# A hybrid attention and retention layer: queries and values stored whole, retention finished every 11 steps instead of 8, output norm weights multiplied on GpSimd

## The chip, the cores and the metric

The kernel runs on one core of one Trainium2 chip. The core has a matrix engine (TensorE, PE in the profile, with its weight loads as PEld), three engines for elementwise work (VectorE, DVE; ScalarE, ACT; GpSimd, POOL), a queue engine that issues transfers (SyncE, SP), and 16 DMA engines between DRAM and SBUF. The metric is the time of one execution on the device, in microseconds (us).

## The reference

One layer over 2048 rows of 1024 numbers, all in float32:

```python
h = rms_norm(x, norm_gain)
q_a, k_a, v_a, g_a, q_r, k_r, v_r, g_r, m_a, m_r = split_columns(h @ w_in)    # 1024 -> 7168
o_a = chunk_band_attention(q_a, k_a, v_a, rel_bias)     # 8 heads of 64, chunks of 64, 8 chunks to the left
branch_a = (o_a * silu(g_a)) @ w_out_attn
o_r = retention_chunkwise(rotary(q_r), rotary(k_r), v_r, gn_gain)   # 8 heads, keys of 64, values of 128
branch_r = (o_r * silu(g_r)) @ w_out_ret
mixed = sigmoid(m_a) * branch_a + sigmoid(m_r) * branch_r
out = rms_norm(x + mixed @ w_out, final_gain)
```

Retention is attention without a softmax: scores of queries and keys times a fixed decay mask, and beside them a running state per head, a 64 x 128 matrix, that is decayed and added to. Its result is normalised for each head.

## The kernel before

**Precision.** A matmul multiplies rounded float32 (fp32r). So an operand is *split*: a high part (an ACT copy that rounds) and a low part (a subtraction of the high part). Three products (high-high, high-low, low-high) stand for one. In names, `wh` and `wl` are the parts of a weight, `sh` and `sl` of masked scores, `o2h` and `o2l` of squares.

**The dense stream.** All projections run as one stream of small *steps*, three matmuls of 128 x 512 each. Blocks are multiplied by a scheme of seven products instead of eight; a product takes four steps, its PSUM tile is `ps_..._x` to `ps_..._z`, and DVE and ACT add these up in tiles `u` and `c` between the products. Weights are loaded on ACT's queue (`raw_g`, `raw_p`), sums of them are made on POOL (`t_g`, `t_p`), split into `wh` and `wl`.

**The stages.** The rows are worked on in two halves. In order: projection 0 (queries, keys and values of half 0), attention 0, retention 0, projection 1, attention 1, retention 1, and a last stage with the two branches' output projections (`ba0`, `br0`, `ba1`, `br1`), the merge, and `out` with the final norm. During attention and retention the gates' projection (`ps_g`) of that half is fed in between: `fill(n)` runs n steps of the dense stream. `later(n, fn)` puts a function off by n steps, `put(n, ...)` a store on SP; `sure()` runs put-off work early where something needs it. Until the last stage each engine works in the order in which the program emits its instructions; in the last stage a scheduler may move those of ACT, DVE and POOL.

**Queries and values on the way.** Projected queries and values are split at once, and both parts go to DRAM (`qrscr` line 176, `vrscr` line 178): `queries` (line 953) by way of `parted` (936), the low part on DVE; `ep_vr` (985) centres the values, then `high` (1003) on ACT and `low` (1007) on POOL.

**Retention** (main loop, lines 1557 to 1589). Heads go in four pairs p, a half's rows in four steps st of 256 rows: 16 units (p, st) per half, each of two heads i. `load_scored` (1373) loads keys and queries of a unit, both parts; `load_valued` (1397) the keys transposed and decayed (`kd`) and the values (`vr`), both parts; `load_state` (1412) takes up the state in half 1. Per head: `scores` (1424) gives `sr` by four matmuls, DVE multiplies by the mask (`sm`), ACT and POOL split it; `output` (1498) adds the products of state and scores into `o`; `evacuate` (1514) copies it out and squares it. Per unit, `update` (1453) multiplies keys and values into `kv`, and `added` (1465) adds it to `state` on DVE; for the first step of a pair ACT copies it there instead. Then ACT rounds the state into `sstk` and DVE adds the low part (1481, 1485). After the last step of half 0 state and sstk are stored (`sts`, `sks`). A fill of about two steps (`RET_FILLS`, line 60) stands between pieces. SBUF tiles come from a pool of 22 buffers.

**Finishing.** `finish_yr` (1071) loads one head's retention output, its gate and its norm factors, multiplies them on DVE and POOL, and stores them (`yrs`) for the branch's projection, which loads them as `r`. For half 1 this happens in the last stage, 16 times, one every `YR_EVERY` steps from step 14 on (lines 65, 66, 1720).

**Output.** `ep_out` (1153) adds the residual on DVE for a half row block of 128 x 512 (`xr`), squares and sums it on ACT, and when both halves are there makes the factor of the norm on DVE and multiplies row factor and norm weights (`fg`) in one DVE operation for each half (1173).

The main loop's body, which sets the order around the change:

```python
if i == 0:
    ops = ps_ret.tile(...)
    if st < 7:
        update(p, st)
    if m + 1 < len(todo):
        load_valued(*todo[m + 1])
        load_state(*todo[m + 1])
fill(RET_FILL)
...
output(p, st, i, parts.pop((p, st, i)), ops)
...
parts[items[n + 2]] = scores(*items[n + 2])
if i == 0 and m + 2 < len(todo):
    load_scored(*todo[m + 2])
fill(RET_FILL)
```

## Time and profile before

| | us |
|---|---|
| three runs: median (lowest, highest) | 1989.13 (1988.7, 1997.05) |
| the profiled execution, as timed | 1994.13 |
| its span in the profile | 1992.3 |
| PE busy in the span | 1927.1 |
| DVE busy | 1362.2 |
| ACT busy | 900.4 |
| POOL busy | 853.0 |

The mean granted clock of the matrix engine was 0.994 of full speed. In this execution retention 0 lies at about 590 to 765 us, projection 1 at 765 to 1105, retention 1 at 1394 to 1560, the last stage from 1560 on.

How to read the lines of the profile: `L140` is the line of a helper that issues most instructions, so that tiles tell them apart; `out<-in` are the tiles written and read. In a timeline a row has its start, its duration, the engine, and in brackets how long the engine idled before it and what ended that. `kv<-vr` is the update, `sr<-qr,kr` the scores, `o<-sh,vr` the output, `sm<-sr,dm` the mask. A wait row names the waiting instruction, what it waited for, and the sum, the number and the longest of these waits.

### The profile page before, as it was taken

Reading aid. Unit: us, or ns where it says so; the run is one execution under the profiler, and the core shown is the slowest. Engines: PE = TensorE matmul, PEld = TensorE weight load, DVE = VectorE, ACT = ScalarE, POOL = GpSimd, SP = SyncE. Lnnn points to the kernel's source line nnn. Section 1 sums busy time; section 2 is a strip of 40 time slices with the busy share of each in tenths; the row PEclk is TensorE's granted clock in tenths of the full one; section 3 lists DMA queues with packets and bytes.
Section 4 is the critical chain, followed back from the end, with each engine's and each line's share of the span. In section 5 each row is a group of like instructions: output and inputs, shape, how many; then the busy total and the mean of one; then the engine's idle time right before and its main releaser. Section 6 shows DMA issues by size and latency. Waiting matters only on the chain.

```text
span 1992.3 us, 30382 instructions
## 1 busy us (share of the span) xinstructions
PE 1927.1 (97%) x9712; PEld 1606.7 (81%) x9712; DVE 1362.2 (68%) x2613; ACT 900.4 (45%) x1827; POOL 853.0 (43%) x703
## 2 busy tenths in 40 slices
PE   6899999999999999999999999999999999999998
PEld 4677788888887877787788888888888887888886
DVE  7887878677765658889887677765557653544554
ACT  6454554566654545443333555654455311322221
POOL 2343544555546665555553444444665144021000
PEclk9999999999999999999999999999999999999999
DMA  4576795756549987687785646554998999976564
GB/s 148 156 265 186 226 307 196 213 153 183 161 132 268 289 243 250 214 289 230 231 277 173 190 150 176 157 144 141 275 285 283 334 377 360 341 242 216 193 193 138
DMA packets 341967, 447.45 MB, mean 225 GB/s; under 512 B 30808, under 2 KB 195312, under 8 KB 341808
## 3 DMA queue, kind: packets, MB, share of 16 engines
q1 hardware_dynamic: 284800, 389.92, 61.3%
q10 hardware_dynamic: 57008, 55.59, 9.2%
q8 instruction: 78, 1.28, 0.3%
q14 instruction: 81, 0.66, 0.1%
HBM read 294.50 MB, written 150.89 MB: 224 GB/s over the span
## 4 chain that ended last, share of the span: by engine, by line
PE 52%; DMA 6%; DVE 6%; issue 2%; POOL 1%; SPq 1%; ACT 0%; DVEq 0%; ACTq 0%; POOLq 0%
PE ps_g_z L140 4%; PE ps_g_x L140 4%; PE ps_p_z L140 3%; PE o L140 2%; PE po L140 2%; PE ps_p_x L140 2%; PE ps_g_v L140 2%; PE ps_g_w L140 2%; PE ps_g_y L140 2%; PE wide L140 2%; PE tp L140 1%; PE ps_p_y L140 1%; PE sr L140 1%; PE ps_p_w L140 1%; PE ps_p_v L140 1%
## 5 line engine op out<-in xcount | busy, mean ns | idle before, releaser
L140 POOL TENSOR_SCALAR pr<-pr,rsum 128x640 f32<-128x640 f32 (+4 forms) x128 | 96.0, 750 | 225.9 <-DVE ptl L140 105.7
L140 PE MATMUL ps_p_z<-r,wh_p 128*128 128x512 f32 x448 | 142.7, 400 | 7.0 <-DVE c_p L140 4.5
L140 PE MATMUL ps_g_z<-r,wh_g 128*128 128x512 f32 x448 | 143.9, 403 | 4.0 <-DVE c_g L140 4.0
L140 PE MATMUL ps_g_x<-r,wh_g 128*128 128x512 f32 x448 | 142.7, 400 | 1.9 <-ACT u_g L140 1.9
L140 PE MATMUL ps_p_x<-r,wh_p 128*128 128x512 f32 x448 | 142.3, 399 | 1.4 <-ACT u_p L140 1.4
L140 DVE CUSTOM_DVE_ANT_0 pr<-wide,bt 128x640 f32<-128x640 f32 (+4 forms) x128 | 94.3, 737 | 71.2 <-PE wide L140 65.4
L140 ACT ACTIVATE pr<-pr,mn 128x640 f32<-128x640 f32 (+4 forms) x128 | 98.0, 766 | 84.9 <-DVE mn L140 84.9
L140 POOL TENSOR_TENSOR t_p<-raw_p,t_p 128x512 f32<-128x512 f32 x50 | 74.5, 1491 | 130.1 <-DVE wl_p L140 114.9
L140 DVE TENSOR_TENSOR ptl<-tp,pth 128x384 fp32r<-128x384 f32 x168 | 96.0, 573 | 40.8 <-ACT pth L140 40.5
L140 ACT CAST pth<-tp 128x384 fp32r<-128x384 f32 x168 | 84.7, 516 | 70.0 <-PE tp L140 64.5
L140 DVE TENSOR_TENSOR wl_p<-t_p,wh_p 128x512 fp32r<-128x512 f32 x112 | 106.4, 951 | 2.0 <-ACT wh_p L140 2.0
L140 POOL TENSOR_TENSOR sl<-sm,sh 128x512 fp32r<-128x512 f32 x64 | 87.7, 1371 | 44.3 <-ACT sh L140 27.5
L1122 POOL TENSOR_TENSOR gr<-gr,ta 128x512 f32<-128x512 f32 x32 | 44.6, 1395 | 141.8 <-DVE gr L1121 133.3
L140 PEld LDWEIGHTS ps_p_z<-r,wh_p 128*128 128x128 f32 x448 | 82.5, 190 | 24.7 <-issue 7.2
L140 PEld LDWEIGHTS ps_p_x<-r,wh_p 128*128 128x128 f32 x448 | 83.8, 190 | 19.9 <-ACT u_p L140 2.2
L140 PE MATMUL wide<-ka,qa 128*128 128x512 f32 (+2 forms) x448 | 94.4, 326 | 2.3 <-DVE mn L140 2.3
L140 DVE TENSOR_TENSOR sm<-sr,dm 128x512 f32<-128x512 f32 x64 | 44.1, 690 | 71.9 <-PE sr L140 41.3
L140 PEld LDWEIGHTS tp<-ident,pr 128*128 128x128 f32 x560 | 71.3, 140 | 27.1 <-POOL pr L140 2.2
L140 POOL TENSOR_TENSOR wl_g<-t_g,wh_g 128x512 fp32r<-128x512 f32 x56 | 75.0, 1339 | 42.3 <-ACT wh_g L140 31.4
L140 PE MATMUL po<-pth,va 128*128 128x256 f32 x336 | 93.1, 298 | 0.0
L140 PE MATMUL tp<-ident,pr 128*128 128x128 f32 x560 | 89.0, 272 | 2.9 <-POOL pr L140 1.6
L140 ACT CAST wh_p<-t_p 128x512 fp32r<-128x512 f32 x112 | 69.1, 619 | 48.1 <-PE ps_p_z L140 19.5
(1184 smaller groups left out, 5879.2 us busy)
## 6 DMA issues: line engine op xcount, KB each, us to landing
raw_g<-in_w_in_dram ACTq DMA_DIRECT2D x56, 512.0 KB, 5.4
raw_p<-in_w_in_dram ACTq DMA_DIRECT2D x50, 512.0 KB, 6.4
qa<-qas SPq DMA_DIRECT2D x128, 128.0 KB, 3.1
qr<-qrs SPq DMA_DIRECT2D x128, 128.0 KB, 4.4
vr<-vrs SPq DMA_DIRECT2D x64, 256.0 KB, 5.3
ka<-kas SPq DMA_DIRECT2D x40, 256.0 KB, 3.7
va<-vas SPq DMA_DIRECT2D x40, 256.0 KB, 3.4
kds<-kdt_k SPq DMA_DIRECT2D x32, 256.0 KB, 4.4
```

The costliest lines, as they stand in the source:

```text
L140: return tc.keep_in_program_order(op(*a, **k))
L1122: pool.tensor_tensor(g, g, ta, ALU.add)
```

## The change

1. Queries and values are stored in DRAM whole, as plain float32, and loaded whole. The split is done in retention: an ACT copy some 7 or 8 steps after the load (`later(8 + more, high)`), a DVE subtraction two steps later, in place for the queries. Queries come as one tile for both heads (`qr`, with the high part `qh`); values as `vr`, split into `v_..._0` and `v_..._1`.
2. In the retention loop values are loaded two units ahead instead of one, and the load positions of queries and values trade places. `update` stands behind the fill, directly ahead of `output`. The first state of a pair is cleared by a POOL memset and then added to like the others; the rounding of the state into `sstk` is on DVE instead of ACT, directly behind the additions.
3. `YR_EVERY` goes from 8 to 11.
4. In `ep_out` POOL multiplies the residual sum by the norm weights beside ACT's square; the row factor is then applied by DVE for one half and by ACT for the other. The sum of the two squares and the added constant become one DVE operation. The last row block's first half is stored from ACT's queue.

The numbers of matmuls are the same, 9698 in both. DVE has 84 instructions more, ACT 29 more, POOL 4 more, SP issues 65 transfers fewer.

```diff
-YR_EVERY = 8
+YR_EVERY = 11
...
-    qrscr = [[D(f"qrs_{c}_{b}", [2, 4, 32, 2, 2, T], F32R) for b in range(NB)] for c in range(2)]
+    qrscr = [[D(f"qrs_{c}_{b}", [2, 2, 32, 2, 2, T]) for b in range(NB)] for c in range(2)]
-    vrscr = [[D(f"vrs_{h}_{b}", [P, 4, 2, DV], F32R) for b in range(NB)] for h in range(HEADS)]
+    vrscr = [[D(f"vrs_{h}_{b}", [P, 4, DV]) for b in range(NB)] for h in range(HEADS)]
...
     def queries(cc, b, xs, nm, late):
-        parted(xs, nm, late + 9, dve, lambda i, h: r32(qrscr[cc][b][:, :, :, h, i]).rearrange("u i c t -> (i c) u t"))
+        def store(n, i):
+            src = xs[n][32 * i:32 * i + 32].rearrange("c (u t) -> c u t", u=2)
+            dma(qrscr[cc][b][:, i // 2, :, n, i % 2].rearrange("u c t -> c u t"), src)
+
+        for n in range(2):
+            for i in range(4):
+                later(late + 8 + PUT + n, lambda n=n, i=i: store(n, i))
...
+                put(PUT, vrscr[h][b], vc)
-            def high():
-                vv.extend(two(f"vr_{nm}", (P, 4, DV)))
-                act.copy(vv[0], vc)
-
-            def low():
-                pool.tensor_tensor(vv[1], vc, r32(vv[0]), ALU.subtract)
-                for n in range(2):
-                    put(PUT, r32(vrscr[h][b][:, :, n, :]), r32(vv[n]))
-
             later(2, centred)
-            later(4, high)
-            later(6, low)
...
-        act.activation(junk, xr, AF.Square, accum_out=fs[:, i:i + 1])
+        act.activation(junk, xr, AF.Square, scale=DM ** -0.5, accum_out=fs[:, i:i + 1])
+        pool.tensor_tensor(fg, xr, fg, ALU.mult)
...
-        dve.tensor_reduce(ft, fs, AX.X, ALU.add)
-        dve.tensor_scalar(ft, ft, 1.0 / DM, NORM_EPS, ALU.mult, ALU.add)
+        dve.scalar_tensor_tensor(ft, fs[:, 0:1], NORM_EPS, fs[:, 1:2], ALU.add, ALU.add)
         rsqrt(ft, fr, tm, hv)
+        dve.tensor_scalar(halves_[1], halves_[1], fr, None, ALU.mult)
+        act.mul(halves_[0], halves_[0], fr)
         for f in range(2):
-            o, fg = halves_[f]
-            dve.scalar_tensor_tensor(o, o, fr, fg, ALU.mult, ALU.mult)
-            put(6, out[0, t * P:(t + 1) * P, 512 * f:512 * f + 512], o)
+            dst = out[0, t * P:(t + 1) * P, 512 * f:512 * f + 512]
+            if t == SEQ // P - 1 and not f:
+                act.dma_start(dst, halves_[f])
+            else:
+                put(6, dst, halves_[f])
...
+            def high():
+                qs.append(E(f"qh_{nm}", F32R, (P, 2, T)))
+                act.copy(qs[0], r32(ql))
+                later(2, low)
+
+            def low():
+                dve.tensor_tensor(ql, r32(ql), r32(qs[0]), ALU.subtract)
+                qs.append(ql)
+
+            later(8 + more, high)
...
+            def high():
+                ws = [E(f"v_{nm}_{i}", F32R, (P, 2, 2 * DV)) for i in range(2)]
+                for i in range(2):
+                    act.copy(ws[i][:, :, 0:DV], raw[:, i])
+                later(2, lambda: low(ws))
+
+            def low(ws):
+                for i in range(2):
+                    dve.tensor_tensor(ws[i][:, :, DV:2 * DV], raw[:, i], r32(ws[i][:, :, 0:DV]), ALU.subtract)
+                vs.extend(ws)
+
+            later(7 + more, high)
...
             def added():
                 for i in range(2):
-                    if st == 0:
-                        act.copy(state[:, i, :], kvv[0:64, i, 0:DV])
-                        continue
...
-                later(3, lambda: high(sstk))
-
-            def high(sstk):
-                act.copy(sstk[0:64], state)
-                later(1, lambda: low(sstk))
-
-            def low(sstk):
+                dve.tensor_copy(sstk[0:64], state)
                 dve.tensor_tensor(sstk[64:128], state, r32(sstk[0:64]), ALU.subtract)
...
-        load_scored(*todo[0])
-        load_valued(*todo[0])
-        load_scored(*todo[1])
+        load_scored(*todo[0], 3)
+        load_valued(*todo[0], 5)
+        load_scored(*todo[1], 5)
         load_state(*todo[0])
+        load_valued(*todo[1], 9)
+        load_scored(*todo[2], 9)
...
-                if st < 7:
-                    update(p, st)
                 if m + 1 < len(todo):
-                    load_valued(*todo[m + 1])
                     load_state(*todo[m + 1])
+                if m and m + 2 < len(todo):
+                    load_scored(*todo[m + 2])
             fill(RET_FILL)
+            if i == 0 and st < 7:
+                if st == 0:
+                    pool.memset(state, 0.0)
+                update(p, st)
...
-            if i == 0 and m + 2 < len(todo):
-                load_scored(*todo[m + 2])
+            if i == 1 and m + 2 < len(todo):
+                load_valued(*todo[m + 2])
             fill(RET_FILL)
```

DVE's order in retention 0, around unit (1, 1) (second head pair, second step), before. `c22`, `u3`, `u2` are sums of the gate projection, `wl` low parts of its weights; the last number of a name only tells tiles apart.

```order
L140 TENSOR_TENSOR c22_g0_9_7664<-ps_g0_9_z_7642,u3_g0_9_7614 128x512
L140 TENSOR_TENSOR wl_g0_10_0_7640<-raw_g0_10_0_7245,wh_g0_10_0_7639 128x512
L140 TENSOR_TENSOR sm_1_1_1_7689<-sr_1_1_1_7676,dm_1_1_7400 128x512
L140 SCALAR_TENSOR_TENSOR state_6975<-state_6975,kv_1_1_7706 64x128 x2
L140 TENSOR_TENSOR state_6975<-kv_1_1_7706,state_6975 64x256 x3
L140 TENSOR_TENSOR u3_g0_9_7614<-ps_g0_9_w_7698,u3_g0_9_7614 128x512
L140 TENSOR_TENSOR wl_g0_10_1_7694<-t2_g0_10_7499,wh_g0_10_1_7693 128x512
L140 TENSOR_TENSOR sm_1_2_0_7763<-sr_1_2_0_7743,dm_1_0_7395 128x512
L140 TENSOR_TENSOR sstk_1_1_7727<-state_6975,sstk_1_1_7727 64x256
```

And the same stretch after the change:

```order
L140 TENSOR_TENSOR c22_g0_9_7595<-ps_g0_9_z_7571,u3_g0_9_7537 128x512
L140 TENSOR_TENSOR wl_g0_10_0_7569<-raw_g0_10_0_7154,wh_g0_10_0_7568 128x512
L140 TENSOR_TENSOR sm_1_1_1_7625<-sr_1_1_1_7607,dm_1_1_7270 128x512
L140 TENSOR_TENSOR v_1_1_0_7588<-vr_1_1_7499,v_1_1_0_7588 128x2x128
L140 TENSOR_TENSOR v_1_1_1_7589<-vr_1_1_7499,v_1_1_1_7589 128x2x128
L140 TENSOR_TENSOR u3_g0_9_7537<-ps_g0_9_w_7634,u3_g0_9_7537 128x512
L140 TENSOR_TENSOR wl_g0_10_1_7630<-t2_g0_10_7418,wh_g0_10_1_7629 128x512
L140 TENSOR_TENSOR qr_1_2_7526<-qr_1_2_7526,qh_1_2_7650 128x512
L140 SCALAR_TENSOR_TENSOR state_6879<-state_6879,kv_1_1_7664 64x128 x2
L140 TENSOR_TENSOR state_6879<-kv_1_1_7664,state_6879 64x256 x3
L140 CAST sstk_1_1_7694<-state_6879 64x256
L140 TENSOR_TENSOR sstk_1_1_7694<-state_6879,sstk_1_1_7694 64x256
```

The low parts of this unit's values and of the next unit's queries have come in around `u3` and `wl`; the state's operations moved behind them, and stand together ahead of the next mask product.

PE's order at the same place, before (`ps_g0_9_w` is a product of the gate projection; two of its dense steps stand between `kv` and `o`):

```order
L140 MATMUL kv_1_1_7706<-vr_1_1_0_7596,kd_1_1_7594 128x256 x2
L140 MATMUL kv_1_1_7706<-vr_1_1_1_7598,kd_1_1_7594 128x256 x2
L140 MATMUL ps_g0_9_w_7698<-r20_85,wh_g0_9_5_7494 128x512
L140 MATMUL ps_g0_9_w_7698<-r21_86,wh_g0_9_5_7494 128x512
L140 MATMUL ps_g0_9_w_7698<-r20_85,wl_g0_9_5_7495 128x512
L140 MATMUL ps_g0_9_w_7698<-r20_85,wh_g0_9_5_7494 128x512
L140 MATMUL ps_g0_9_w_7698<-r21_86,wh_g0_9_5_7494 128x512
L140 MATMUL ps_g0_9_w_7698<-r20_85,wl_g0_9_5_7495 128x512
L140 MATMUL o_1_1_7705<-qr_1_1_0_7520,sstk_1_0_7610 128x256 x2
L140 MATMUL o_1_1_7705<-sh_1_1_0_7654,vr_1_1_0_7596 128x256
```

And after, from the last matmul of that product to the scores of the next unit:

```order
L140 MATMUL ps_g0_9_w_7634<-r20_85,wl_g0_9_5_7414 128x512
L140 MATMUL kv_1_1_7664<-v_1_1_0_7588,kd_1_1_7502 128x256 x2
L140 MATMUL kv_1_1_7664<-v_1_1_1_7589,kd_1_1_7502 128x256 x2
L140 MATMUL o_1_1_7643<-qh_1_1_7517,sstk_1_0_7563 128x256
L140 MATMUL o_1_1_7643<-qr_1_1_7398,sstk_1_0_7563 128x256
L140 MATMUL o_1_1_7643<-sh_1_1_0_7582,v_1_1_0_7588 128x256
L140 MATMUL o_1_1_7643<-sl_1_1_0_7618,v_1_1_0_7588 128x256
L140 MATMUL o_1_1_7643<-sh_1_1_0_7582,v_1_1_0_7588 128x256 x2
L140 MATMUL o_1_1_7643<-sl_1_1_0_7618,v_1_1_0_7588 128x256
L140 MATMUL o_1_1_7643<-sh_1_1_0_7582,v_1_1_0_7588 128x256
L140 MATMUL sr_1_2_0_7679<-qh_1_2_7650,kr_1_2_7523 128x256
L140 MATMUL sr_1_2_0_7679<-qr_1_2_7526,kr_1_2_7523 128x256
```

The update's four matmuls moved from ahead of the two dense steps to behind them; the scores now need `qh` first and the low query, `qr`, second.

More of the change, by code (lines that the diff above doesn't have):

```diff
@@ L1371, in retention, with load_scored @@
         begun = [False]
-        def load_scored(p, st):
+        def load_scored(p, st, more=0):
             b, un = st // 2, st % 2
@@ L1384, in load_scored, with load_valued @@
                 )
-            for i in range(2):
-                q = E(f"qr_{nm}_{i}", F32R, (P, 2, T))
-                for half in range(2):
-                    dma(
-                        r32(q[64 * half:64 * half + 64]),
-                        r32(qrscr[cc][b][un, 2 * (p % 2) + i]).rearrange("c h n t -> (c h) n t"),
-                    )
-                qs.append(q)
-                if st == 4 * s:
+            ql = E(f"qr_{nm}", F32R, (P, 2, T))
+            for half in range(2):
+                dma(
+                    r32(ql[64 * half:64 * half + 64]),
+                    qrscr[cc][b][un, p % 2].rearrange("c h i t -> (c h) i t"),
+                )
+            if st == 4 * s:
+                for i in range(2):
                     load_mask(p, i)
+            qs = []
             tiles[p, st] = ks, qs
-        def load_valued(p, st):
+            def high():
[6 more added lines that the diff above has]
+            later(8 + more, high)
+        def load_valued(p, st, more=0):
             b, un = st // 2, st % 2
             nm = f"{p}_{st}"
+            raw = E(f"vr_{nm}", shape=(P, 2, 2, DV))
+            for i in range(2):
+                dma(raw[:, i], vrscr[2 * p + i][b][:, 2 * un:2 * un + 2])
             kd = E(f"kd_{nm}", F32R, (P, 2, T))
@@ L1403, in load_valued @@
             vs = []
-            for i in range(2):
-                v = E(f"vr_{nm}_{i}", F32R, (P, 2, 2 * DV))
-                dma(
-                    r32(v), r32(vrscr[2 * p + i][b][:, 2 * un:2 * un + 2]).rearrange("p t n d -> p t (n d)")
-                )
-                vs.append(v)
-            values[p, st] = vs, kd.rearrange("p i (t c) -> p i t c", t=2)
+            values[p, st] = vs, kd.rearrange("p i (t c) -> p i t c", t=2)
+            def high():
+                ws = [E(f"v_{nm}_{i}", F32R, (P, 2, 2 * DV)) for i in range(2)]
+                for i in range(2):
+                    act.copy(ws[i][:, :, 0:DV], raw[:, i])
+                later(2, lambda: low(ws))
+            def low(ws):
+                for i in range(2):
+                    dve.tensor_tensor(ws[i][:, :, DV:2 * DV], raw[:, i], r32(ws[i][:, :, 0:DV]), ALU.subtract)
+                vs.extend(ws)
+            later(7 + more, high)
         def load_state(p, st):
@@ L1422, in load_mask, with sure @@
             dma(dms[p][i], dmask[2 * p + i])
+        def sure(here):
+            while not here():
+                emit()
         def scores(p, st, i):
@@ L1431, in scores @@
                 kcol = ks[:, i, kk * P:(kk + 1) * P]
-                pe.matmul(o, kcol, qs[i][:, 0, :], start=True, stop=False)
-                pe.matmul(o, kcol, qs[i][:, 1, :], start=False, stop=True)
+                pe.matmul(o, kcol, qs[0][:, i, :], start=True, stop=False)
+                pe.matmul(o, kcol, qs[1][:, i, :], start=False, stop=True)
             got = []
@@ L1455, in update @@
             vs, kd = values[p, st]
+            sure(lambda: len(vs) == 2)
             kv = ACC(f"kv_{p}_{st}")
@@ L1491, in update @@
             later(1, added)
-        def sure(here):
-            while not here():
-                emit()
         def output(p, st, i, parts, ops):
@@ L1500, in output @@
             o = ops[:, i * T:(i + 1) * T]
-            sure(lambda: len(parts) == 2 and (st == 0 or (p, st) in sstks))
+            sure(lambda: len(parts) == 2 and len(vs) == 2 and (st == 0 or (p, st) in sstks))
             sh, sl = parts
@@ L1504, in output @@
                 sstk = sstks[p, st]
-                pe.matmul(o, sstk[:, i, :], qs[i][:, 0, :], start=True, stop=False)
-                pe.matmul(o, sstk[:, i, :], qs[i][:, 1, :], start=False, stop=False)
+                pe.matmul(o, sstk[:, i, :], qs[0][:, i, :], start=True, stop=False)
+                pe.matmul(o, sstk[:, i, :], qs[1][:, i, :], start=False, stop=False)
             for kk in range(2):
```

5 lines of the change are left out of this document (2 added, 3 removed).

## The prediction

> **What bounds the kernel now.** I read the page's totals first, then the stretches of the stages, then PE's waits in each stage, then single places in the timeline. The page:
>
> ```profile
> span 1992.3 us, 30382 instructions
> PE 1927.1 (97%) x9712; PEld 1606.7 (81%) x9712; DVE 1362.2 (68%) x2613; ACT 900.4 (45%) x1827; POOL 853.0 (43%) x703
> ```
>
> PE is busy for 97%, and the change takes no matmul away. So all that can be won is PE's idle time, 1992.3 − 1927.1 = 65 us, and only where its cause goes. The stretches of retention 0, retention 1, projection 1 and the running part of projection 0 (length, then busy time of PE, PEld, DVE, ACT, POOL with counts, PE's clock, DMA share, GB/s):
>
> ```profile
> 600.00:765.00 165.00, 156.36 (x904) 134.77 (x903) 96.81 (x173) 84.14 (x164) 102.40 (x78) 0.99 0.84 253
> 1394.00:1560.00 166.00, 164.78 (x950) 142.65 (x950) 104.96 (x174) 86.34 (x161) 97.44 (x72) 1.00 0.92 284
> 765.00:1105.00 340.00, 330.46 (x1495) 269.07 (x1495) 291.51 (x375) 136.85 (x257) 179.90 (x122) 0.99 0.76 244
> 75.00:360.00 285.00, 280.13 (x1306) 228.11 (x1305) 223.08 (x318) 140.84 (x307) 126.42 (x86) 0.99 0.74 237
> ```
>
> PE idles 165.00 − 156.36 = 8.6 us in retention 0, only 1.2 us in retention 1, 9.5 us in projection 1, 4.9 us in projection 0. DVE is at 59%, 63% and 86% in the first three, POOL at 62% and 59% in the two retentions. What PE waits for in retention 0 (us in all, times, longest):
>
> ```profile
> PE ps_g_z L140 <- DVE c_g L140: 2.1, 1, 2.1
> PE ps_g_x L140 <- ACT u_g L140: 1.9, 2, 1.2
> PE o L140 <- POOL sl L140: 1.7, 3, 1.0
> PE kv L140 <- DMA vr<-vrs: 1.3, 2, 0.8
> PE ssq L140 <- POOL o2l L140: 1.1, 1, 1.1
> PE o L140 <- ACT o L140: 0.5, 1, 0.5
> ```
>
> They sum to the 8.6. In the last stage PE has one such wait:
>
> ```profile
> PE ps_br_(0, 0)_18880 L140 <- ACT wh_br_(0, 0)_18803 L296: 2.2, 1, 2.2
> ```
>
> **What goes in retention 0.** The longest wait is a chain that the timeline shows:
>
> ```profile
> 720.59 0.42 ACT L140 COPY state<-kv 64x128 f32<-64x128 f32 x2 [3.82 <-DMA sts<-state]
> 721.04 1.33 DVE L140 TENSOR_TENSOR state<-kv,state 64x256 f32<-64x256 f32 x3 [5.29 <-ACT state L140]
> 722.41 0.69 DVE L140 TENSOR_TENSOR c_g<-ps_g_z,u_g 128x512 f32<-128x512 f32 x1
> ```
>
> ACT's copy of the first state waits 3.82 us for the store of the last head pair's state, DVE waits 5.29 us for ACT with c_g behind it, and PE's next product behind c_g. In the changed kernel a POOL memset takes the copy's place, and the update stands behind the dense fill instead of ahead of it, some 2 us later. The memset still waits for that store, so what is late next is POOL's queue (sl behind the memset); with 3.82 against some 2 us later, I count the 2.1 us as gone (bounds 0 and 2.1). The vr waits (1.3) go: values arrive two units ahead instead of one. The u_g waits (1.9) go in part with the state copies and sstk casts that leave ACT; of the other 3.3 (sl, o2l, o), POOL and ACT queues, about half. 2.1 + 1.3 + 1.9 + 1.2 = **−6.5** (0 to −8.6). Retention 1: **−0.5** (0 to −1.2).
>
> **What DVE gains in work there.** Rows of retention 0 (busy us, mean ns) and, from the projections, the old query subtraction and a subtraction of 256 columns:
>
> ```profile
> L140 DVE TENSOR_TENSOR sm<-sr,dm 128x512 f32<-128x512 f32 x32 | 22.1, 690 | 41.6 <-PE sr L140 21.4 <-DMA ors<-oz 9.6 <-PE kv L140 6.1
> L140 DVE TENSOR_TENSOR wl_g<-raw_g,wh_g 128x512 fp32r<-128x512 f32 x15 | 13.5, 898 | 0.0
> L140 DVE TENSOR_TENSOR wl_g<-t_g,wh_g 128x512 fp32r<-128x512 f32 x10 | 9.7, 970 | 0.0
> L140 DVE SCALAR_TENSOR_TENSOR state<-state,kv 64x128 f32<-64x128 f32 x24 | 5.7, 274 | 8.5 <-PE kv L140 8.5
> L140 POOL TENSOR_TENSOR sl<-sm,sh 128x512 fp32r<-128x512 f32 x32 | 43.0, 1344 | 20.6 <-ACT sh L140 13.6 <-PE o L140 3.4 <-DMA qr<-qrs 2.5
> L140 DVE TENSOR_TENSOR l_q<-u_p,h_q 128x512 fp32r<-128x512 f32 x8 | 5.4, 679 | 0.0
> L140 DVE TENSOR_TENSOR kdt_k<-trkr_k,kdt_k 128x256 fp32r<-128x256 f32 x32 | 12.3, 413 | 0.0
> ```
>
> New per half: 16 query subtractions × 0.68 = 10.9; 32 value subtractions × 0.41 = 13.1; 16 casts of sstk (12 in half 1), whose DVE form the trace lacks, between 0.27 (state 64x128) and 0.41, say 0.3 = 4.8; 8 state operations × 0.27 = 2.2. In all 31 us: DVE goes from 97 to 128 us of 165. It has room on the mean; the order decides. As the order pieces show, the query subtraction now stands between the last dense operations and the scores. Two neighbouring rows on each engine give the rates:
>
> ```profile
> 924.23 0.68 DVE L140 TENSOR_TENSOR xq<-xq,t_q 128x512 f32<-128x512 f32 x1
> 924.83 1.78 DVE L140 TENSOR_TENSOR u_p<-u_p,cs_q 128x512 f32<-128x512 f32 x1
> 924.38 1.68 POOL L140 TENSOR_TENSOR t_p<-raw_p,raw_p 128x512 f32<-128x512 f32 x1 [4.24 <-DVE wl_p L140]
> 717.69 0.28 PE L140 MATMUL o<-sh,vr 128*128 128x256 f32 x1
> 717.81 0.28 PE L140 MATMUL o<-sl,vr 128*128 128x256 f32 x1
> ```
>
> DVE starts one such operation per 0.60 us, PE one matmul of 256 columns per 0.12. At the place in the order pieces PE does 4 kv, 8 o and 1 sr after ps_w, 13 × 0.117 = 1.5 us, and then needs the low query; DVE does u3, wl and the query meanwhile, 3 × 0.60 = 1.8: 0.3 short. By the same count over the 32 queries, retention 0 has eight tight places (slack −0.55, −0.32, −0.32, 0.13, 0.36, 0.36, 0.36, 0.52 us), retention 1 three (0.36, 0.52, 0.58). Hand-overs (0.69 against 0.60 at DVE's end, 0.28 against 0.12 at PE's) take 0.25 off each: 0.80 + 0.57 + 0.57 + 0.12 = 2.1 us without collisions. But the three rows above also show that u_p, with both inputs in SBUF, took 1.78 instead of 0.68 while POOL's t_p ran, and ended with it. wl_g, the same kind, means 0.90 and 0.97 in retention 0, so a collision costs 0.22 to 0.29 each on the mean; wl and the query together, 0.5 a place: 1.3 + 1.07 + 1.07 + 0.62 + 3 × 0.39 + 0.23 = 5.5 in retention 0, and 0.4 + 0.2 + 0.2 in retention 1. **+6.3**; bounds 2 (no collision) and 26 (both operations pushed by the full 1.1 at all eleven places, 11 × 2.2 + 2).
>
> The Trainium skill, "SBUF — State Buffer", section "SBUF: two separate sides", says that the port pair which DVE and GpSimd share is an exclusive lock: a DVE operation with two SBUF inputs and a GpSimd operation that reads SBUF block each other for a whole instruction. Row 924.83 agrees. It speaks against this change, since it turns a push of 0.25 into one that grows with POOL's share. If each DVE operation met POOL at a random moment, it would wait 0.62 × 1.34 / 2 = 0.42 on the mean, and two of them 0.84 a place: 8.2 + 1.7 = 10 us instead of 6.3. I take the measured means of wl_g, the nearest operation, for the sum and leave the rest to the last rival.
>
> **Projections.** 16 l_q (11 us of DVE), 32 high parts on ACT and 32 low parts on POOL leave. DVE's 86% in projection 1 makes its queue matter, but most of its idle PE stands behind the rotary products, ahead of l_q. **−2** (0 to −6).
>
> **DMA and the merge.** Loads, KB each and time to landing:
>
> ```profile
> qr<-qrs SPq DMA_DIRECT2D x128, 128.0 KB, 4.4
> vr<-vrs SPq DMA_DIRECT2D x64, 256.0 KB, 5.3
> ```
>
> 128 × 131 KB and 64 × 262 KB, 16.8 MB each, halve. PE waits 1.3 us for values in retention 0 and 1.2 for everything in retention 1, so this alone is worth no more than the terms above. On SP the value loads move ahead by half a unit and more, past stores (ors, gates), and a unit holds seven SBUF buffers of the 22 instead of six, so a load may wait for a buffer with those stores queued behind it. Nobody on PE needs the stores in the stage, and the loads have two units, 2 × 165 / 16 = 20 us, for 4.4 to 5.3 us of landing: 0; were that cover gone, it would be the vr waits again, 1.3. The later finishes matter at one place:
>
> ```profile
> 1655.40 0.62 ACT L296 CAST wh_br_(0, 0)_18803<-raw_br 128x512 fp32r<-128x512 f32 x1 [15.28 <-DMA raw_br<-in_w_out_ret_dram]
> 1640.00:1680.00 40.00, 37.82 (x161) 30.78 (x160) 16.51 (x23) 3.54 (x7) 18.45 (x15) 0.96 1.02 371
> 1676.72 0.47 SPq L140 DMA_DIRECT2D yrs<-yr  x1
> 1720.50 0.32 SPq L140 DMA_DIRECT2D r<-yrs  x1
> ```
>
> The 16 engines are full there (share 1.02) and the weight comes late, so PE waits 2.2. A step is three dense matmuls of 512 columns, twice 0.117 each, 0.70 us. A finish every 11 steps is one per 7.7 instead of 5.6 us, which takes some pressure off: **−2** (0 to −2.2). The last of the 16 finishes moves 15 × 3 = 45 steps back, 32 us, and its store (the first of the last two rows) from 1677 to 1709; the load that needs it (the other) starts at 1720.5 and stands at the same dense step. Its cover falls from 44 to 12 us, which still hides it; gone, every microsecond beyond it would be PE's.
>
> **The tail.** The chain behind the last matmul:
>
> ```profile
> 1985.06 0.63 ACT L1164 ACTIVATE jk<-xr 128x512 bf16<-128x512 f32 x1 [4.66 <-DVE xr L1158]
> 1985.81 0.15 DVE L1168 TENSOR_REDUCE f<-fs 128x1 f32<-128x2 f32 x1 [0.79 <-ACT jk L1164]
> 1986.00 0.15 DVE L1169 TENSOR_SCALAR f<-f 128x1 f32<-128x1 f32 x1
> 1987.91 1.41 DVE L1173 SCALAR_TENSOR_TENSOR xr<-xr,f,fg 128x512 f32<-128x512 f32 x2
> L140 DVE TENSOR_SCALAR xa<-xa,n_a 128x512 f32<-128x512 f32 x7 | 3.1, 483 | 0.1
> ```
>
> One small operation less (0.19), and instead of 1.41 for two products, 0.48 on DVE beside one on ACT (0.7 at most, as a 512-column ACT cast takes 0.62): 0.7 + 0.19 = **−0.9** (−0.7 to −1.1). POOL's multiplication (1.34) runs beside the square and the chain (1985.06 to 1987.9), so it costs nothing; without that cover 1.3.
>
> **Sum.** −6.5 − 0.5 − 2 − 2 − 0.9 + 6.3 = −5.6. The profiled execution took 1994.13 us (span 1992.3 and 1.8 around it); it becomes 1988.5. The three runs have a median of 1989.13, 5 us less, and I set the difference against that: 1983.5, say **1984**.
>
> **The rivals.** *DVE keeps ahead (faster).* If the tight places cost only the 2.1 us, as they do where POOL happens to run elsewhere, the gains stay: −11.9 + 2.1 = −10, and with all gains at their ends −19.1 + 2 = −17. Middle −13: 1976. For it: in retention 1 PE loses only 1.2 us beside a DVE at 63%, and only three of its places are tight. Against: three in retention 0 are short with no collision at all.
>
> *DVE and POOL hold each other up (slower).* DVE's 128 us become 140 with 48 new operations pushed by 0.25, and 165 × 0.85 is reached; each low query then comes behind a full queue, PE waits at the scores, sm comes later, sl later, and o waits. At the 26 us bound: −11.9 + 26 = +14, 2003 us. It decides against the change from 22 us on, 0.5 us at each of the 32 queries beyond what I counted. For it: wl_g means 0.97 where the free xq row shows 0.68. Against: at the mean push DVE still idles 25 us in the half. The page's lock, named above, would make this case likelier.
>
> *Nothing happens.* PE is the bound, transfers were hidden, and the gains above are replaced by the same waits under other names: −1 (the tail alone), 1988.
>
> **Chances.** A change below 0.5%, 9.9 us, is about what a measurement of this kernel can't tell from none. Forecast near balance 0.36 and nothing happens 0.08, both inside it: 0.44. DVE ahead, 0.36. Slower, 0.20. The range leaves out the best end of the second and the worst of the third: 1971 to 2003; the likeliest case alone, 1979 to 1994.
>
> **What would show it.** Right: in retention 0 the waits for vr and the 2.1 for c_g gone; PE waiting for the low query at the scores a few tenths at a time, 6 us in both halves; DVE near 128 us of its 165; the 2.2 at ps_br gone; span's end 0.9 us nearer the last matmul. Wrong: PE idle over 20 us in a retention, sm or wl_g over 1.1 us on the mean, or the projections changing by more than 6 us.

## The result and the profile after

The changed kernel takes 2003.81 us (median of 5 runs, 2002.09 to 2006.84); the kernel before took 1989.13 (5 runs, 1988.03 to 1997.05). The ratio is 1.0068, with a 95% interval of [1.0047, 1.0089]: slower by some 14 us, where 1984 was forecast and 1971 to 2003 given. The profiled execution has a span of 2005.1 us against 1992.3, 12.8 more. The page's first lines after the change:

```profile
span 2005.1 us, 30311 instructions
PE 1932.8 (96%) x9712; PEld 1609.6 (80%) x9712; DVE 1431.2 (71%) x2697; ACT 908.2 (45%) x1855; POOL 861.0 (43%) x707
```

PE has as many instructions as before, 9712. DVE is busy for 69 us more. To see where the time went I cut both spans at the same events: a retention runs from the last score matmul of the attention before it (`wide`) to its own last sum of squares (`ssq`).

| stage (us) | before | after | difference | forecast |
|---|---|---|---|---|
| projection 0 and attention 0 | 570.8 | 569.4 | −1.4 | −2 for both projections |
| retention 0 | 192.3 | 201.7 | +9.4 | −6.5 + 5.5 |
| projection 1 and attention 1 | 597.3 | 596.1 | −1.2 | (in the first row) |
| retention 1 | 197.3 | 205.3 | +8.0 | −0.5 + 0.8 |
| last stage | 426.2 | 424.1 | −2.1 | −2 |
| behind the last matmul | 8.4 | 8.5 | +0.1 | −0.9 |

So all that was lost was lost in the two retentions, 17.4 us, and some of it came back elsewhere. Their stretches, first of the kernel before, then of the changed one (length, busy PE, PEld, DVE, ACT, POOL, then PE's clock, DMA share, GB/s):

```profile
570.80:763.10 192.30, 183.54 (x1046) 157.78 (x1045) 109.56 (x200) 96.07 (x187) 114.83 (x89) 0.99 0.78 233
1360.40:1557.70 197.30, 195.10 (x1107) 167.93 (x1106) 118.90 (x204) 101.35 (x189) 113.47 (x85) 1.00 0.84 258
```
```profile
569.40:771.10 201.70, 186.70 (x1047) 159.22 (x1046) 165.34 (x272) 105.25 (x211) 120.60 (x93) 0.99 0.58 180
1367.20:1572.50 205.30, 197.94 (x1106) 169.98 (x1105) 159.59 (x264) 115.04 (x225) 117.93 (x85) 0.98 0.67 208
```

DVE's busy time grows by 55.8 and 40.7 us, where 31 was forecast: 82% and 78% of the stage. Of the 17.4 us, 11.4 are idle time of PE (15.0 instead of 8.8 us, and 7.4 instead of 2.2); 6.0 are longer busy time for the same matmuls (3.2 and 2.8). The DMA share falls, 0.78 to 0.58 and 0.84 to 0.67, and PE loses only waits of 1.3 and 1.0 us for loads with it. What PE waits for in retention 0, then in retention 1, after the change:

```profile
PE sr L140 <- DVE qr L140: 8.8, 9, 2.1
PE kv L140 <- DVE v L140: 2.4, 3, 0.9
PE o L140 <- ACT o L140: 1.5, 2, 1.3
PE o L140 <- POOL sl L140: 1.2, 1, 1.2
...
PE sr L140 <- DVE qr L140: 3.8, 2, 3.3
PE ps_g_x L140 <- ACT u_g L140: 2.2, 2, 1.8
```

The old waits for `vr` and `c_g` are gone, as forecast; in their place PE waits for the two new subtractions, `qr` above all. The place of the order pieces, unit (1, 1), in the timeline (DVE's u3, wl and low query, POOL's o2l and sl, PE's scores):

```profile
654.79 0.69 DVE L140 TENSOR_TENSOR u_g<-ps_g_w,u_g 128x512 f32<-128x512 f32 x1 [0.24 <-PE ps_g_w L140]
655.39 1.13 DVE L140 TENSOR_TENSOR wl_g<-t_g,wh_g 128x512 fp32r<-128x512 f32 x1
656.45 1.75 DVE L140 TENSOR_TENSOR qr<-qr,qh 128x512 fp32r<-128x512 f32 x1
...
654.68 1.29 POOL L140 TENSOR_TENSOR o2l<-o,o2h 128x512 fp32r<-128x512 f32 x1 [0.75 <-ACT o2h L140]
655.94 1.71 POOL L140 TENSOR_TENSOR sl<-sm,sh 128x512 fp32r<-128x512 f32 x1
...
658.26 0.38 PE L140 MATMUL sr<-qr,kr 128*128 128x256 f32 x1 [1.95 <-DVE qr L140]
```

The four operations take turns. o2l ends at 655.97, wl 0.55 later; sl starts with wl still running, takes 1.71 instead of 1.3 and ends at 657.65; the low query, started at 656.45, ends 0.55 after that, at 658.20. It needed 0.68 alone. The Trainium skill's "SBUF — State Buffer", section "SBUF: two separate sides", describes just this, a lock held for a whole instruction by one of the two engines; the rows agree. Not every unit meets it: of the 16 low queries of retention 0, seven took 0.68 or 0.69 us, five 1.11 to 1.39, and four 1.75 or 1.76, each of these with POOL's sl running beside it. PE's waits behind those four, 1.74, 1.95, 2.11 and 1.26 us, are 7.1 of the 8.8. The groups of DVE in retention 0:

```profile
L140 DVE TENSOR_TENSOR v<-vr,v 128x256 fp32r<-128x256 f32 x32 | 22.7, 749 | 1.6 <-ACT v L140 1.6
L140 DVE TENSOR_TENSOR wl_g<-raw_g,wh_g 128x512 fp32r<-128x512 f32 x18 | 19.9, 1104 | 0.0
L140 DVE TENSOR_TENSOR qr<-qr,qh 128x512 fp32r<-128x512 f32 x16 | 18.1, 1133 | 5.6 <-ACT qh L140 5.6
L140 DVE CAST sstk<-state 64x256 fp32r<-64x256 f32 x16 | 9.7, 609 | 0.6
```

All four were costed lower: 0.41, 0.93, 0.93 (0.68 and a push of 0.25, the time that another engine's operation adds) and 0.3 us.

The longest wait, in retention 1, is of another kind:

```profile
1545.17 1.16 DVE L140 TENSOR_TENSOR r<-r,r 128x512 fp32r<-128x512 f32 x1
1546.25 0.68 DVE L140 TENSOR_TENSOR wl_ba_(0, 0)_17646<-raw_ba,wh_ba_(0, 0)_17645 128x512 fp32r<-128x512 f32 x1
1546.86 0.68 DVE L140 TENSOR_TENSOR r<-r,r 128x512 fp32r<-128x512 f32 x1
1547.46 0.68 DVE L140 TENSOR_TENSOR qr<-qr,qh 128x512 fp32r<-128x512 f32 x1
...
1548.19 0.58 PE L140 MATMUL sr<-qr,kr 128*128 128x256 f32 x1 [3.31 <-DVE qr L140]
```

The low query itself ran its 0.68 us. It was late because it stood at the end of a queue on which DVE had worked without a gap since 1536, with splits of operands (`r`, `wl_ba`) for the products to come ahead of it. Behind this wait PE's clock was halved (the columns of the stretches again):

```profile
1548.10:1554.30 6.20, 6.11 (x16) 4.78 (x17) 4.88 (x13) 1.66 (x3) 0.05 (x1) 0.50 0.33 114
```

From 1536.0 to 1544.8 it had been 1.00. At 0.50 for 6.2 us, this adds an estimated 3.1 us to a wait of 3.3, though PE looks busy: it is about what PE's busy time grew by in retention 1. The 3.2 us of retention 0 aren't accounted for: the clock was at 0.50 there too, from 677.4 to 680.4, but so it was in the kernel before, from 724.8 to 726.8.

### The profile page after: what moved, and what is told of

It is laid out like the page before. It is cut to its first block, busy times and chain, and to the rows that moved or that the text cites. A ratio compares the mean times of both kernels' runs of the same rounds, so it can differ in the third digit from the quotient of the medians.

```text
span 2005.1 us, 30311 instructions
## 1 busy us (share of the span) xinstructions
PE 1932.8 (96%) x9712; PEld 1609.6 (80%) x9712; DVE 1431.2 (71%) x2697; ACT 908.2 (45%) x1855; POOL 861.0 (43%) x707
## 4 chain that ended last, share of the span: by engine, by line
PE 72%; DVE 13%; DMA 8%; issue 3%; ACT 2%; SPq 1%; POOL 1%; DVEq 0%; ACTq 0%; POOLq 0%
PE ps_g_x L140 6%; PE ps_g_z L140 6%; PE ps_p_x L140 5%; PE ps_p_z L140 5%; PE po L140 4%; PE wide L140 3%; PE ps_g_v L140 3%; PE ps_g_y L140 3%; PE ps_g_w L140 3%; PE tp L140 2%; PE ps_p_y L140 2%; PE ps_p_v L140 2%; PE o L140 2%; PE ps_p_w L140 2%; DVE wl_p L140 2%
## 5 line engine op out<-in xcount | busy, mean ns | idle before, releaser
L140 DVE TENSOR_TENSOR ptl<-tp,pth 128x384 fp32r<-128x384 f32 x168 | 95.9, 572 | 40.7 <-ACT pth L140 40.1
L140 DVE TENSOR_TENSOR wl_p<-t_p,wh_p 128x512 fp32r<-128x512 f32 x112 | 101.6, 908 | 1.6 <-ACT wh_p L140 1.6
L1160 POOL TENSOR_TENSOR fg<-xr,fg 128x512 f32<-128x512 f32 x32 | 43.6, 1362 | 129.2 <-DVE xr L1154 110.9
```

Source lines behind the costliest of these rows:

```text
L140: return tc.keep_in_program_order(op(*a, **k))
L1160: pool.tensor_tensor(fg, xr, fg, ALU.mult)
```

## The experiments

Two theories at first. *Collision*: the low query meets POOL's o2l and sl just where the scores need it. *Queue*: DVE simply has too much to do, in any order. The rival to both was that the moved update and state cost the time (*state theory*). After the first runs the two became *filled DVE* (the splits fill DVE, POOL pushes them, and the waits come up at the next hand-over), and at the end *queue* against *push*: DVE's order, or the lock that DVE and POOL share. All ratios are to the kernel before, run beside each on the same chip, 5 rounds.

| run | us (median) | ratio [95%] | retention 0, 1 (us, profiled) |
|---|---|---|---|
| changed kernel | 2003.81 | 1.0068 [1.0047, 1.0089] | 201.7, 205.3 |
| queries split as before | 1996.17 | 1.0018 [1.0004, 1.0032] | 190.2, 204.2 |
| values split as before | 2000.26 | 1.0042 [1.0028, 1.0056] | 197.7, 202.0 |
| both split as before | 1989.29 | 0.9976 [0.9965, 0.9986] | 186.5, 205.3 |
| no o2l | 1994.53 | 1.0013 [1.0002, 1.0023] | 197.0, 202.2 |
| kernel before, no o2l | 1990.07 | 0.9980 [0.9969, 0.9991] | 185.3, 195.4 |
| low query two steps earlier | 2004.29 | 1.0061 [1.0046, 1.0077] | 200.0, 208.0 |
| update and state as before | 2028.14 | 1.0170 [1.0153, 1.0187] | 226.2, 204.3 |
| no low query | 1988.83 | 0.9980 [0.9966, 0.9994] | 189.2, 200.9 |
| no low values | 1998.94 | 1.0040 [1.0028, 1.0052] | 197.7, 202.5 |
| neither low part | 1983.57 | 0.9957 [0.9944, 0.9971] | 182.9, 198.3 |
| both split, o2l on DVE | 2002.33 | 1.0055 [1.0040, 1.0070] | 189.4, 205.9 |
| low query on POOL | 2009.69 | 1.0080 [1.0066, 1.0093] | 199.9, 209.4 |
| the same, values split | 2000.90 | 1.0032 [1.0020, 1.0043] | 195.5, 203.4 |
| before with rhythm and output | 1990.98 | 0.9992 [0.9980, 1.0004] | 190.1, 197.7 |

A single profiled execution can lie some us from the median (both split: span 1994.4, median 1989.29), so a stage's length is read as a hint and the ratio as the verdict. Costs of single parts are differences of two ratios, so they are uncertain by 3 to 5 us.

**Queries split as before, and values split as before.** The parts of the change on the one, then on the other, are taken back. Of the first:

```diff
-    qrscr = [[D(f"qrs_{c}_{b}", [2, 2, 32, 2, 2, T]) for b in range(NB)] for c in range(2)]
+    qrscr = [[D(f"qrs_{c}_{b}", [2, 4, 32, 2, 2, T], F32R) for b in range(NB)] for c in range(2)]
...
+            for i in range(2):
+                q = E(f"qr_{nm}_{i}", F32R, (P, 2, T))
...
-                pe.matmul(o, kcol, qs[0][:, i, :], start=True, stop=False)
+                pe.matmul(o, kcol, qs[i][:, 0, :], start=True, stop=False)
```

> The changed kernel with the queries as before: split in the projection, both parts in DRAM, loaded as two parts; all else of the change kept. Collision theory (the low query is pushed by POOL's o2l and sl just where the scores need it): PE's waits of sr for qr (8.8 us in retention 0, 3.8 in retention 1, plus 2.4 of slower matmuls behind the longest) go, DVE is 18 and 15 us less busy there: 1990 us, from 1987 to 1993. Queue theory (DVE has too much to do there in all, collision or not): the same 1990. Rival, the moved update and state work on DVE cost the time: waits of sr stay or turn into waits for state and values: 1997 or more.

> The changed kernel with the values as before: split in the projection, both parts loaded, but two units ahead as in the change. Collision theory: the waits of kv for v (2.4 us in retention 0) go, and the waits of sr for the low query stay near 8 us in retention 0, since the low query meets o2l at the same place: 1999 us (1997 to 2002). Queue theory: DVE has 45 us less to do in the two halves, the low query is done earlier, and its waits fall below 4: 1994 us or less.

Split queries bring 1.0018, split values 1.0042. In retention 0 with split queries, then with split values, PE's waits are:

```profile
PE o L140 <- ACT sh L140: 2.9, 1, 2.9
PE kv L140 <- DVE v L140: 2.2, 4, 0.9
PE o L140 <- POOL sl L140: 1.0, 1, 1.0
```
```profile
PE sr L140 <- DVE qr L140: 7.0, 6, 2.6
PE o L140 <- POOL sl L140: 1.8, 2, 1.0
...
```

The waits for the low query go with it; but they shrink little when DVE loses the values' 23 us (7.0 against 8.8), as collision expects and queue doesn't. With split queries 1.0018 is at the upper end of the expected 1987 to 1993, so this run alone doesn't tell whether the queries are all of it. Its longest wait, the 2.9 for sh, is a late load: ACT waits 3.5 us there for values, with sh behind.

**Both split as before.** The two edits above together.

> The changed kernel with queries and values both split in the projection as before; what is left of the change in retention is the update behind the fill, the memset, the rounding of the state on DVE and the load positions; the rhythm of 11 and the new output stay. Filled-DVE theory (the splits fill DVE, POOL pushes them, and PE's waits come up wherever the next hand-over is): both retentions back at 192 and 197 us, give or take 2; with 2 less in the last stage the time is 0.999 of the kernel before. State theory (the moved update and the state's rounding on DVE cost most): retention 1 stays at 202 us or more, and the time is 1.002 of before or more.

0.9976: faster than the kernel before, and than the changed one. So the update behind the fill, the state on DVE, the load positions, the rhythm and the output together gain some 5 us, and the state theory's time, 1.002 or more, is out. From this run to the changed kernel the queries whole cost 0.0066 (13 us, the run with values split against this one), the values whole 0.0042 (8 us), both 0.0092 (18 us). Its retention 1 was no shorter than the changed kernel's in the profiled execution, against the expectation of 197 ± 2; it is what the state theory said of that stage, but in the slowest execution of twelve, so the share of the moves there isn't told apart.

**Update and state as before**, with queries and values whole:

```diff
-                dve.tensor_copy(sstk[0:64], state)
+                later(3, lambda: high(sstk))
...
+                if st < 7:
+                    update(p, st)
```

> The changed kernel with update, first copy and rounding of the state as before (update ahead of the fill, both copies on ACT); queries and values stay whole. Filled-DVE theory: DVE loses 9 to 12 us in each half, its waits shrink in part: retention 0 at 197 to 200 us, retention 1 at 200 to 203, 1.003 to 1.005 of before. State theory: retentions within 2 us of before (192, 197), 0.999 of before.

Neither: 1.017, the slowest of all. DVE has less to do (149 us in retention 0 instead of 165), and yet PE waits more for it:

```profile
PE sr L140 <- DVE qr L140: 21.2, 11, 4.1
PE kv L140 <- DVE v L140: 7.2, 8, 1.7
```

So DVE's sum of work is not the whole of it. With the update ahead of the fill the state's additions stand ahead of the low query, and at four places they wait for ACT's copy (8.5 us of DVE's waits in that stage are for it), with the low query queued behind: PE's waits of 4.1 and 3.5 us at the scores follow DVE's waits of 3.8 and 3.0 for the copy. The clock adds to it: its mean in this stage is 0.95, and PE is busy for 196.3 us instead of 186.7. In retention 0 the moves that I had as a rival cause are what keeps the whole queries bearable; retention 1 is as long without them (204.3).

**Low query two steps earlier.**

```diff
-                later(2, low)
+                later(1, low)
...
-            later(8 + more, high)
+            later(7 + more, high)
```

> The changed kernel with the query's high part one step earlier after its load and the low part two steps earlier, so that DVE does it ahead of the last sum of the gate projection instead of behind it. Collision and queue theory: the waits of sr for the low query fall to 2 us or less in both halves: 1992 us (1989 to 1996). Rival, the load or ACT's high part is what comes late (ACT waited 6.0 us for the load of queries in retention 0, DVE 5.6 for ACT): ACT waits longer for the load, what is behind it on ACT comes late, and the time stays at 2000 or more.

The wait at the scores goes in retention 0, and the time stays at 1.0061, so both theories' 1992 was wrong and the rival's 2000 or more came:

```profile
PE o L140 <- ACT sh L140: 3.9, 1, 3.9
PE o L140 <- ACT o L140: 2.8, 3, 1.8
...
PE sr L140 <- DVE qr L140: 0.4, 1, 0.4
```
```profile
602.79 0.68 DVE L140 TENSOR_TENSOR sm<-sr,dm 128x512 f32<-128x512 f32 x1
...
606.18 0.62 ACT L140 CAST qh<-qr 128x512 fp32r<-128x512 f32 x1 [3.50 <-DMA qr<-qrs]
606.70 1.13 ACT L140 CAST sh<-sm 128x512 fp32r<-128x512 f32 x2
...
607.37 0.58 PE L140 MATMUL o<-sh,v 128*128 128x256 f32 x1 [3.87 <-ACT sh L140]
```

The mask product sm is done at 603.5. The query's high part now stands ahead of sh on ACT; it waits 3.5 us for its load, sh waits behind it, and PE waits 3.9 for sh and 0.8 more for sl. (In the changed kernel ACT waits 2.9 us for this load too, but sh is done before.) The clock is at 0.50 from 606.9 to 612.6 behind that, an estimated 2 us more. In retention 1 ACT waits 2.9 us for the load in the same way, and PE 1.4 for sh and 1.0 for sl. So the run took the late low query away and put a late load in its place; it doesn't tell what the place of the operation costs.

**No o2l, in the changed kernel and in the kernel before.** Both sums of squares take the high part twice:

```diff
-                got.append(E(f"o2l_{nm}", F32R))
-                pool.tensor_tensor(got[1], o2, r32(got[0]), ALU.subtract)
+                got.append(got[0])
```

> The changed kernel without POOL's subtraction for the low part of the squares (o2l); the sums of squares take the high part twice instead, so that part of the computation is left out. DVE's work and order stay. Collision theory: the low query's subtraction, 1133 ns on the mean in retention 0, falls below 850, and the waits of sr for it from 8.8 us to 4 or less: 1996 us (1993 to 1999). Queue theory: within 2 us of the changed kernel, 2002 to 2005.

> The kernel before without POOL's low part of the squares, as in the run on the changed kernel; that part of the computation is left out. Where DVE is not full, POOL's o2l costs nothing: only the one wait of 1.1 us for it goes, 0.9995 of before, each retention within 2 us. If leaving it out helps the kernel before as much as the changed one (8 us in the two retentions), the run on the changed kernel said nothing on collisions with the new work: 0.996 of before.

Leaving out 32 POOL operations wins 0.0055 (11 us) in the changed kernel and 0.0020 (4 us) in the kernel before, more there than I expected. So some 7 of the 11 (2 to 12 by the intervals) come only together with DVE's new work. The low query falls from 1133 to 993 ns, not to the 850 expected, and the waits for it from 8.8 to 5.7 us, not to 4.

**No low query, no low values, neither.** Scores and output take the high query twice; update and output the high values twice; loads and ACT's copies stay:

```diff
-                dve.tensor_tensor(ql, r32(ql), r32(qs[0]), ALU.subtract)
-                qs.append(ql)
+                qs.append(qs[0])
...
-                for i in range(2):
-                    dve.tensor_tensor(ws[i][:, :, DV:2 * DV], raw[:, i], r32(ws[i][:, :, 0:DV]), ALU.subtract)
...
-                        kv[:, i * 256:(i + 1) * 256], kd[:, i, kk, :], vs[i][:, kk, :],
+                        kv[:, i * 256:(i + 1) * 256].rearrange("p (n d) -> p n d", n=2), kd[:, i, kk, :],
+                        vs[i][:, kk, None, 0:DV].broadcast_to([P, 2, DV]),
...
-                pe.matmul(o, v4[:, DV:2 * DV], sh[:, c], start=False, stop=(kk == 1))
+                pe.matmul(o, v4[:, 0:DV], sh[:, c], start=False, stop=(kk == 1))
```

> The changed kernel without DVE's subtraction for the low query: scores and output take the high query twice, so that part of the computation is left out; loads, ACT's copies and all else stay. Theory (DVE's new work, pushed by POOL, is what PE waits for): retention 0 near the 190 us of the run with split queries, 1.001 of before (0.999 to 1.003). Rival (ACT's new copies and the wait for the loads cost the time): PE waits for ACT's qh instead, 1.005 or more.

> The changed kernel without DVE's subtraction for the low values: update and output take the high values twice, so that part of the computation is left out; loads, ACT's copies and all else stay. Theory: as with split values, 1.004 of before (1.002 to 1.006), PE's waits for the low query stay near 7 us in retention 0. Rival (ACT's copies and loads): no better than the changed kernel, 1.0065.

> The changed kernel with neither of the two subtractions on DVE, both left out of the computation as in the two runs for one of them. Theory: DVE's busy share in retention falls to that of the run with both split, and the time with it: 0.9975 of before (0.996 to 0.999). Rival (ACT's 21 us of new copies in each half and later loads have a share): 1.001 or more.

0.9980, 1.0040 and 0.9957; the first and the last are better than expected. The 16 subtractions of queries in each half cost 0.0088 (17.5 us), the 32 of values 0.0028, both 0.0111 (22 us): more than the change lost. ACT's 48 new copies a half and the later loads, which stay, cost no more than the rest of the change saves; the rival falls. With neither, retention 0 is down to 182.9 us, with DVE at 69%:

```profile
568.30:751.20 182.90, 181.08 (x1046) 157.15 (x1045) 126.86 (x224) 104.61 (x210) 116.53 (x93) 1.00 0.65 198
```

Whole data in DRAM would be worth 0.0019 against the run with both split (the intervals overlap), if the split cost nothing.

**Low query on POOL**, then the same with the values split:

```diff
-                dve.tensor_tensor(ql, r32(ql), r32(qs[0]), ALU.subtract)
+                pool.tensor_tensor(ql, r32(ql), r32(qs[0]), ALU.subtract)
```

> The changed kernel with the low query made on POOL instead of DVE; nothing is left out. Queue theory (the place in DVE's full queue costs, and POOL, with 40 us of idle time a half more than DVE's, has room): near the run without the low query, 1.000 of before (0.997 to 1.002), and it beats the changed kernel by 10 us or more. Push theory (two engines on one port: what counts is the sum of both engines' SBUF work, whoever does it): POOL is 21 us longer busy in each half, pushes DVE's other operations as much, sl and o2l come later, and PE waits for sl and for the low query on POOL: 1.005 or more.

> The same with the values split as before: queries whole in DRAM, their low part on POOL. Queue theory: 4 to 8 us below the run with values whole, 0.996 of before (0.994 to 0.998), which would beat both kernels. Push theory: 1.001 or more.

1.0080 and 1.0032: no gain, as the push theory has it, against the queue theory's 1.000 and 0.996. It isn't a clean separation: on POOL such a subtraction takes 1.35 us on the mean, and PE waits 4.2 us in retention 0 for low queries in POOL's queue. DVE's groups in retention 0 with the low query on POOL:

```profile
L140 DVE TENSOR_TENSOR v<-vr,v 128x256 fp32r<-128x256 f32 x32 | 27.4, 897 | 4.4 <-ACT v L140 4.3
...
L140 DVE CAST sstk<-state 64x256 fp32r<-64x256 f32 x16 | 13.8, 865 | 0.6
```

The other new operations stretch, 749 to 897 and 609 to 865 ns. DVE is rid of 18.1 us of queries, yet only 8.9 less busy (165.3 to 156.4), and POOL is 19.3 us more.

**Both split, o2l on DVE.**

```diff
-                pool.tensor_tensor(got[1], o2, r32(got[0]), ALU.subtract)
+                dve.tensor_tensor(got[1], o2, r32(got[0]), ALU.subtract)
```

> The run with queries and values both split, and the low part of the squares (o2l) made on DVE instead of POOL: a version that may beat both kernels. If POOL's pushes cost more than DVE's time at this fill (16 operations of 0.7 us a half): 0.996 of before, below the 0.9976 of the run with both split. If DVE's fill decides: 0.998 or more.

1.0055, 16 us more than the run with both split, for 16 operations of 0.8 us a half. The rows point at DVE's order: o2l waits there for PE and ACT (9.7 us in retention 0) with DVE's other work behind it, and PE waits 4.0 us for o2l. But they don't hold the 16 us: this profile is of the fastest of six executions (1997.07 us), the one with both split of the slowest of twelve, and their two retentions differ by 3.5 us.

**The rhythm of 11 and the new output alone**, on the kernel before:

> The kernel before with the rhythm of 11 and the new output alone. By the stages of the changed kernel: last stage 2 us shorter, end of the chain no shorter (8.4 us): 0.999 of before, 1987 us where before takes 1989.

0.9992, not told apart from 1, as expected; the last stage took 423.9 us instead of 426.2.

## Why the prediction was wrong, point by point

**The failed term.** It is the +6.3 us for "What DVE gains in work there". Whole queries and values cost 18 us (both split against the changed kernel), and their subtractions on DVE alone 22 (the run with neither low part against the changed kernel). In the main the mechanism was the one named, the low query late at the scores through POOL's pushes and DVE's queue: PE waited 8.8 and 3.8 us there, where 5.5 and 0.8 were forecast. Of the signs of being wrong that the prediction named none came clearly: PE's idle time, 15.0 us, stayed under 20, and wl_g was at 1.10 us for its 18 rows from raw_g but at 1.02 with the 12 others. The term's size was off, in four ways that the rows show.

1. *The new operations.* 31 us of DVE work a half were forecast; DVE's time grew by 56 and 41, with 52 and 45 in the new operations. I had priced the values by a row that reads PSUM (0.41) where the new operation reads SBUF twice (0.75), the rounding of the state at 0.3 instead of 0.61, and the query at a push of 0.25 instead of 0.45.
2. *Pushes are no random meeting.* In four units of retention 0 the low query started beside POOL's sl and took 1.75 us, and four fifths of the waits stand there; in seven it took its 0.68. I took the mean over wl_g, which stands everywhere. The prediction's sum by the Trainium skill's lock, 8.2 us for retention 0's waits, came nearer to the 8.8 measured than my 5.5. The rows agree with the lock; that the sum is so near is in part luck, since it took the meetings as random. Its 1.7 for retention 1 (1.8 by the slacks given) was below the 3.8, where the 3.3 came from DVE's queue without a push of the low query.
3. *Waits move.* I added up places as if each were alone. Taking the waits at the scores away (8.8 to 0.4 us) raised those at `o` from 2.7 to 7.9, 4.6 of them behind a load that the earlier query outran. The eight tight places were a list for one hand-over only; kv (2.4 us in retention 0) and the gate's products (2.2 in retention 1) had to be counted too.
4. *PE's clock.* A wait of 3.3 us cost an estimated 3.1 more; nothing of it was in the sum.

**The gains.** The waits for vr and c_g went as forecast, yet the two retentions' −7.0 wasn't reached: both split against the rhythm and output alone is 0.0016, some 3 us. With neither low part it is 0.0035, 7 us, which is the sum forecast for the two retentions; but that includes what the projections save. All gains together were −11.9 in the forecast and −8.6 in that run (0.9957). Projections: −2 forecast, −1.4 and −1.2 in the first and third rows of the stages. Last stage: −2 forecast, −2.1, and the wait of 2.2 at ps_br is gone. Tail: −0.9 forecast, +0.1, because POOL's multiplication was no free cover:

```profile
1997.85 1.26 POOL L1160 TENSOR_TENSOR fg<-xr,fg 128x512 f32<-128x512 f32 x1 [4.20 <-DVE xr L1154]
1998.50 0.62 DVE L1165 SCALAR_TENSOR_TENSOR f<-fs 128x1 f32<-128x1 f32 x1 [0.79 <-ACT jk L1159]
...
2000.94 0.72 ACT L1168 ACTIVATE fg<-fg,f 128x512 f32<-128x512 f32 x1 [2.47 <-DVE f L205]
...
2001.69 0.37 ACTq L1172 DMA_DIRECT2D out_dram<-fg  x1
```

An operation on one column took 0.62 us and ended with POOL's (1999.12 and 1999.11), where the two operations that it replaces took 0.15 each. The end of the arithmetic came nearer to the start of the last sum (4.64 us behind it instead of 4.99), but the end of the span did not (8.1 us behind it instead of 8.0): the last store, issued on ACT's queue at 2001.69, takes the 0.35 us back; the span ends 3.4 us behind its issue.

**The rivals.** "DVE and POOL hold each other up" is in the main what happened, at 2003 us against 2003.8; it had 0.20. The last link of its chain, `o` waiting for sl, stayed as it was (1.2 us in retention 0 against 1.7), so its time is nearer than its account. Its argument against, that DVE would still idle 25 us a half, was no protection: 36 us of idle were left in retention 0 and PE waited all the same. The range ended where this case's one time stood, at 2003, though its price was an estimate with bounds of its own.

**Open.** How the 18 us divide between POOL's pushes and DVE's order isn't settled. The pushes are shown row by row, and some 7 us of them by the two runs without o2l; the run with the state as before and retention 1's longest wait show the order; the run with the low query on POOL shows that neither engine had room for it. Where the run with o2l on DVE loses its 16 us is not shown. Nor is why retention 1 keeps 198 us or more in every run with the moved update, against 197.3 before.

## What to carry to other kernels

An engine that idles 40% of its stage isn't free for 20% more: what it does at a hand-over is late by all that stands ahead of it. Before such an operation is moved ahead, see that its input has landed by then: here it outran its load, and the wait came back elsewhere. Price a new VectorE operation by a row with the same operands in the same memory, and look what GpSimd does at that very place, not on the mean. Work that another stage did under cover (the split in the projection) can be dearer in a stage where three engines pass each tile on.

## What the runs showed of the hardware

DVE's rounding of the state has one input in SBUF, and I had expected pushes only for two. In retention 0 after the change it took 284 to 1234 ns (lowest, middle, highest):

```profile
L140 DVE CAST sstk<-state x16: 284/744/1234, 612.3 to 762.0; 64x256 fp32r<-64x256 f32 x16
```

Its mean of 609 fell to 558 ns without POOL's o2l and rose to 865 with the low query on POOL. The Trainium skill's section on the two sides, named above, counts a copy of one input in a two-port mode among those that take the lock; no run here shows in which mode the rounding ran.

PE's clock fell to half behind a wait of 3.3 us (0.50 for 6.2 us), and in the kernel before behind the wait of 2.1 at c_g (0.50 from 724.8 to 726.8) and of 2.2 at ps_br:

```profile
1656.10:1659.50 3.40, 3.40 (x9) 2.63 (x10) 2.61 (x5) 1.66 (x3) 0.59 (x1) 0.53 1.05 395
```

Behind the waits of 1.7 to 2.1 us in retention 0 after the change it stayed at 1.00 (646.9 to 653.0, 658.2 to 664.5, 729.9 to 736.0). Yet two waits of 0.8 and 0.9 us with two matmuls between them halved it:

```profile
675.64 0.50 PE L140 MATMUL kv<-v,kd 128*128 128x256 f32 x2 [0.77 <-DVE v L140]
677.06 0.72 PE L140 MATMUL kv<-v,kd 128*128 128x256 f32 x2 [0.91 <-DVE v L140]
677.40:680.40 3.00, 3.00 (x15) 3.00 (x15) 2.62 (x8) 0.00 (x0) 3.00 (x3) 0.50 0.04 15
```

So the length of a single wait doesn't tell what the clock will do. The Trainium skill's "TensorE: Matmul & The Clock Gate", section "Part 1: The HAM clock gate (the "warmup" mystery)", gives an idle window of about 3.4 us, free-running, as what halves the clock. The 3.3 us come near it; the 2.1 and 2.2 us, and the 0.8 and 0.9, are shorter than it states, and no run here shows why they sufficed.
